# Odd layer's windowed attention: score products split into three float32r matmuls, the two heads alternating on the row halves, and the maps normalised on VectorE

## The chip, the cores and the metric

The program runs on one core of one Trainium2 chip. The metric is the device time of one execution in microseconds (us), lower is better. The engines are named as in the profile: PE (TensorE matmul), PEld (its weight load), DVE (VectorE), ACT (ScalarE), POOL (GpSimd) and SP (SyncE, whose queue issues most transfers).

## The reference

One step of a two-layer trunk over 128 context tokens and 256 latent tokens of 1024 features, in float32. The odd layer's mixer, which the change touches, is a windowed attention with 16 query heads, 4 key and value heads of 64 features, and one extra logit per head (the sink):

```python
q, k, v = jnp.split(h @ w_in, [...], axis=-1)
q = _rms_norm(q.reshape(b, s, C_HEADS, HEAD_DIM), qk_g[0])
k = _rms_norm(k.reshape(b, s, C_KV_HEADS, HEAD_DIM), qk_g[1])
...
s_c = jnp.einsum("bqgrd,bcgd->bgrqc", qi, k_ctx) * scale      # cached context keys
s_l = jnp.einsum("bqgrd,bkgd->bgrqk", qi, ks) * scale         # latent keys, rotated
s_l = jnp.where(valid, s_l, -jnp.inf)                         # |query - key| <= 128
p = jax.nn.softmax(jnp.concatenate([s_c, s_l, sink], axis=-1), axis=-1)
o = p_c @ v_ctx + p_l @ v_lat
```

Context tokens attend only to their own 128 keys. The rest of each layer is two half SwiGLU blocks and, in the even layer, another attention; none of that is changed.

## The kernel before

All 384 tokens stay on the chip, feature-major. Weights stream in tiles of up to 1 MB through the SP queue into three `raw` buffers and are split into a high and a low float32r part (`wh` by ACT, line 80; `wl` by DVE or POOL, line 84). A projection is then three float32r matmuls for each 128 rows (`mm3`, lines 178 to 180). The odd mixer has a start and a pipeline.

**The start.** `odd_mixer` makes keys and the first queries (u = 0), then the values, then rotates the two key tiles `kt[0]`, `kt[1]` (`finish_keys`) and copies them with their halves of the partitions swapped into `kt[2]`, `kt[3]` by four transfers. Then it rotates the first queries (`rope`, four DVE instructions, lines 706 to 710) and calls `advance(8)`. `advance` runs pieces of the products of the other queries (u = 1, 2, 3, each with two chunks c); a finished product is squared and copied by ACT (`hsq`, `oq`, lines 721 and 722), its rows of sums are made by PE (`rows`, line 679), brought to columns (`cols`, line 691), and its latent part is rotated.

**The pipeline.** It has 24 steps (u, c, i): two query heads, which lie on the two halves of the partitions, and one tile i of 128 queries. For i = 0 there are 128 keys, for i = 1 and 2 there are 384; three steps with the same u and c are called a triple here. In the program's order, step s has: the scores of s on PE (`s`, line 1202, and a mask added by a matmul with an identity, line 1208); on DVE two maxima `omx` (line 1214), then `ong`, `oes` (lines 1216 to 1222) and for the step before `ors` (lines 1234, 1235); on ACT two exponentials `e` (line 1226) and `oes`; on POOL the product of the maps of s - 1 with their factors (line 1236); `fill(s)`, which is pieces of the query products, and from step 18 of the output product `down`; the transposes `aT` of s - 3 (line 1246) and their copies `at_sb` on ACT (line 1248); the products `oo` with the values for s - 4 (line 1259), which after i = 2 are split into `gh` (ACT, line 1266) and `gl` (DVE, line 1267); and half a weight tile of splitting (`refill_half`). Each engine works through its own list in this order, which is fixed when the program is built.

## Time and profile before

| what | value |
|---|---|
| time, median of 3 runs | 1532.3 us (1532.04 to 1536.19) |
| span of the profiled execution | 1533.8 us |
| its mean granted TensorE clock | 0.989 |
| PE busy, DVE busy, ACT busy, POOL busy | 1496.8, 1087.1, 665.4, 188.5 us |
| first score matmul of the odd layer, first `oo` | 1117.0 us, 1133.9 us |
| last score matmul, last `oo` | 1207.1 us, 1220.7 us |

The profiled execution's span is 1.5 us above the median of the timed runs. Times within the execution are counted from the start of its span. A busy PE is not a PE at its peak, since matmuls are pipelined and their ends are modelled.

### The profile page before, as it was taken

What the parts mean: (1) busy time and instruction counts of PE and PEld (TensorE: products, weight loads), DVE (VectorE), ACT (ScalarE), POOL (GpSimd) and SP (SyncE); (2) the same over time, 40 slices, a digit from 0 to 9 for tenths busy, and PEclk for the clock granted to TensorE, in tenths of its full rate; (3) what the DMA queues carried; (4) which work ended last, traced back from release to release, by engine and by line L of the source; (5) the groups of instructions that cost most, each with busy time, mean ns of one, the idle gap of its engine ahead of it and who ended that gap; (6) DMA issues with size and microseconds to landing.
All of it is one profiled execution on the core that took longest, in us unless ns stands there. A gap on an engine that the chain in (4) does not pass through costs nothing.

```text
span 1533.8 us, 22554 instructions
## 1 busy us (share of the span) xinstructions
PE 1496.8 (98%) x8938; PEld 1419.5 (93%) x8938; DVE 1087.1 (71%) x1723; ACT 665.4 (43%) x1218; POOL 188.5 (12%) x120
## 2 busy tenths in 40 slices
PE   7989999999999999999999999999999999999998
PEld 5888999999899999999999999999965799999998
DVE  2799888868786887787779868876785386444432
ACT  3653333366555642334454333325565564232331
POOL 2450000005322100000010000000453230000000
PEclk9999999999999999999999999999997999999999
DMA  9767677642323376576536656743320034433431
GB/s 292 233 221 234 226 242 259 220 151 90 110 83 124 116 255 220 179 246 221 178 110 218 223 179 222 243 165 111 109 74 29 4 111 137 138 98 127 142 102 41
DMA packets 204555, 248.60 MB, mean 162 GB/s; under 512 B 5957, under 2 KB 186786, under 8 KB 204450
## 3 DMA queue, kind: packets, MB, share of 16 engines
q1 hardware_dynamic: 203374, 245.79, 48.6%
q8 instruction: 70, 1.15, 0.3%
q10 hardware_dynamic: 1076, 1.38, 0.3%
q14 instruction: 35, 0.29, 0.1%
HBM read 244.26 MB, written 2.36 MB: 161 GB/s over the span
## 4 chain that ended last, share of the span: by engine, by line
PE 85%; DVE 7%; ACT 3%; issue 2%; POOL 1%; DMA 1%; SPq 0%; ACTq 0%; DVEq 0%; POOLq 0%
PE proj L178 17%; PE proj L180 17%; PE proj L179 17%; PE down L179 8%; PE down L178 8%; PE down L180 8%; PE s L1202 2%; DVE wl L84 2%; PE m_sum L269 1%; PE oo L1259 1%; ACT wh L80 1%; PE aT L1246 1%; DVE acc L354 1%; DVE macc L228 1%; DVE x L359 1%
## 5 line engine op out<-in xcount | busy, mean ns | idle before, releaser
L178 PE MATMUL proj<-xh,wh 128*128 128x384 f32 (+1 forms) x1648 | 562.8, 342 | 1.1 <-ACT xh L391 1.1
L179 PE MATMUL proj<-xl,wh 128*128 128x384 f32 (+1 forms) x1648 | 556.8, 338 | 2.3 <-DVE xl L463 2.2
L180 PE MATMUL proj<-xh,wl 128*128 128x384 f32 (+1 forms) x1648 | 556.1, 337 | 0.0
L84 DVE TENSOR_TENSOR wl<-raw,wh 128x1024 fp32r<-128x1024 f32 (+1 forms) x292 | 352.6, 1246 | 131.2 <-ACT wh L80 130.6
L80 ACT ACTIVATE wh<-raw 128x1024 fp32r<-128x1024 f32 (+1 forms) x330 | 317.3, 1012 | 150.9 <-PE down L179 81.8
L178 PEld LDWEIGHTS proj<-xh,wh 128*128 128x128 f32 x1648 | 310.4, 188 | 16.2 <-issue 9.5
L179 PEld LDWEIGHTS proj<-xl,wh 128*128 128x128 f32 x1648 | 310.9, 189 | 3.6 <-DVE xl L463 3.2
L180 PEld LDWEIGHTS proj<-xh,wl 128*128 128x128 f32 x1648 | 310.4, 188 | 0.0
L178 PE MATMUL down<-gh,wh 128*128 128x384 f32 x832 | 280.8, 337 | 8.2 <-ACT gh L628 8.2
L179 PE MATMUL down<-gl,wh 128*128 128x384 f32 x832 | 279.3, 336 | 1.6 <-DVE gl L629 1.6
L180 PE MATMUL down<-gh,wl 128*128 128x384 f32 x832 | 278.6, 335 | 0.0
L221 DVE SCALAR_TENSOR_TENSOR macc<-wm,cpad,macc 128x1024 f32<-128x1024 f32 x210 | 259.1, 1278 | 0.3 <-issue 0.3
L178 PEld LDWEIGHTS down<-gh,wh 128*128 128x128 f32 x832 | 156.4, 188 | 11.6 <-ACT gh L628 8.8
L179 PEld LDWEIGHTS down<-gl,wh 128*128 128x128 f32 x832 | 156.4, 188 | 3.6 <-DVE gl L629 3.3
L180 PEld LDWEIGHTS down<-gh,wl 128*128 128x128 f32 x832 | 156.4, 188 | 0.0
L628 ACT ACTIVATE gh<-gf 128x768 fp32r<-128x768 f32 x44 | 37.3, 848 | 262.2 <-DVE gf L618 256.9
L359 DVE SCALAR_TENSOR_TENSOR x<-down,m,x 128x128 f32<-128x128 f32 x224 | 82.5, 411 | 72.9 <-PE down L180 72.9
L611 ACT ACTIVATE sg<-proj 128x384 f32<-128x384 f32 x78 | 37.8, 488 | 147.2 <-PE proj L180 147.1
L84 POOL TENSOR_TENSOR wl<-raw,wh 128x1024 fp32r<-128x1024 f32 (+1 forms) x38 | 82.7, 2189 | 134.1 <-ACT wh L80 105.4
L618 DVE TENSOR_TENSOR gf<-proj,sg 128x384 f32<-128x384 f32 x78 | 43.2, 554 | 68.4 <-PE proj L180 68.4
L189 POOL TENSOR_TENSOR nr<-nv,neghalf 128x3 f32<-128x3 f32 x6 | 5.1, 853 | 573.0 <-DVE nv L418 573.0
L629 DVE TENSOR_TENSOR gl<-gf,gh 128x768 fp32r<-128x768 f32 x44 | 42.2, 958 | 40.2 <-ACT gh L628 40.2
(212 smaller groups left out, 1168.5 us busy)
## 6 DMA issues: line engine op xcount, KB each, us to landing
raw<-in_ffn_w SPq DMA_DIRECT2D x117, 1024.0 KB, 5.3
wm<-in_w_mod SPq DMA_DIRECT2D x128, 512.0 KB, 4.1
raw<-in_ffn_w SPq DMA_DIRECT2D x16, 768.0 KB, 5.9
raw<-in_even_w_in SPq DMA_DIRECT2D x12, 1024.0 KB, 5.2
wm<-in_w_mod SPq DMA_DIRECT2D x24, 256.0 KB, 6.1
raw<-in_odd_w_in SPq DMA_DIRECT2D x6, 1024.0 KB, 4.8
raw<-in_even_w_out SPq DMA_DIRECT2D x4, 1024.0 KB, 5.0
raw<-in_odd_w_out SPq DMA_DIRECT2D x4, 1024.0 KB
```

What stands on the lines that cost most here:

```text
L80: self.k.nc.scalar.activation(parts[0][:, a:b], raw[:, a:b], AF.Copy)
L84: engine.tensor_tensor(out=lo[:, a:b], in0=raw[:, a:b], in1=h[:, a:b].bitcast(F32), op=ALU.subtract)
L178: mm(out, w[0], x[0], start=first, stop=False)
L179: mm(out, w[0], x[1], start=False, stop=False)
L180: mm(out, w[1], x[0], start=False, stop=last)
L221: nc.vector.scalar_tensor_tensor(out=acc, in0=t, scalar=c, in1=acc, op0=ALU.mult, op1=ALU.add)
L359: self.nc.vector.scalar_tensor_tensor(out=self.x[oc][:, a:b], in0=psum[:, a:b], scalar=gate[:, oc, g:g + 1], in1=self.x[oc][:, a:b], op0=A ...
L611: nc.scalar.activation(sg[c], out[:, 0:T], AF.Silu)
L618: nc.vector.tensor_tensor(out=gf[:, c], in0=out[:, 0:T], in1=sg[c], op=ALU.mult)
L628: nc.scalar.activation(gh[:, at:at + 2], gf, AF.Copy)
L629: nc.vector.tensor_tensor(out=gl[:, at:at + 2], in0=gf, in1=gh[:, at:at + 2].bitcast(F32), op=ALU.subtract)
L1202: nc.tensor.matmul(s[p][:, 0:n], qs[u][hs, c, i * P:(i + 1) * P], keys[p][hs, k0:k0 + n], start=True, stop=(i == 0),)
```

## The change

The queries and keys of the odd layer's attention are split into float32r parts. `kh`, `kl` hold the two key tiles, `kh2`, `kl2` the swapped ones; each query product goes to a scratch tile (`oqf`, for u = 0 `q0`), is rotated there, and then ACT writes its high part (line 1105 of the new kernel) and DVE its low part (line 1106); `key_parts` does the same for keys (lines 1178, 1179). The score of a step is then three float32r matmuls for each head, in an order that alternates between the two heads, and both masks follow behind them (lines 1230, 1237). The maps are multiplied by their factors with two DVE instructions (line 1266) and no longer on POOL. The four swapping transfers are issued from the SP queue. `fill` calls `advance(1)` in every step, the output product begins at step 17 and goes on at every other step, and the new keys' output (`nk`) is made ahead of the pipeline. The parts lie in buffers that the modulation's stream used; for this the accumulator `macc` moves to another pool.

```diff
     def odd_mixer(self, l):
         okt = self.mix.tile([P, 4, 512], F32, tag="kt", name="okt")
         kt = [okt[:, i] for i in range(4)]
+        kh, kl, kh2 = [self.wpool.tile([P, 2, 512], F32R, tag="wm", name="okp", bufs=3) for _ in range(3)]
+        kl2 = self.wpool.tile([P, 2, 512], F32R, tag="wp", name="okp", bufs=1)
...
-        qs[0] = self.mix.tile([P, 2, T], F32, tag="q", name="oq", bufs=2)
-        sqq = [self.first_squares(tiles[2 + j], self.odd_g[:, 0:1], qs[0][:, j], j) for j in range(2)]
+        def query_tiles(u):
+
+            if u == 2:
+                t = self.mix.tile([P, 2, 2, T], F32R, tag="kt", name="oq")
+                return [t[:, 0], t[:, 1]]
+            pool, tag = (self.wpool, "macc") if u == 1 else (self.mix, "q")
+            return [pool.tile([P, 2, T], F32R, tag=tag, name="oq", bufs=2) for _ in range(2)]
+
+        def query_parts(u, c, t):
+            h, lo = qs[u]
+            nc.scalar.activation(h[:, c], t, AF.Copy)
+            nc.vector.tensor_tensor(out=lo[:, c], in0=t, in1=h[:, c].bitcast(F32), op=ALU.subtract)
+
+        q0 = [self.c3("q0"), self.c3("q0")]
+        sqq = [self.first_squares(tiles[2 + j], self.odd_g[:, 0:1], q0[j], j) for j in range(2)]
...
             yield from self.project_pieces(c, res, 2)
-            sq = self.scaled_and_squares(res[0], self.odd_g[:, 0:1], qs[u][:, c], c)
+            full[u, c] = self.c3("oqf")
+            sq = self.scaled_and_squares(res[0], self.odd_g[:, 0:1], full[u, c], c)
...
             def rope(u, c):
-                self.rope(qs[u][:, c, TC:T], qs[u][:, c, TC:T])
+                t = full.pop((u, c))
+                if c == 0:
+                    qs[u] = query_tiles(u)
+                self.rope(t[:, TC:T], t[:, TC:T])
+                query_parts(u, c, t)
...
         for j in range(2):
             self.finish_keys(ksc[:, j], rk, j, kt[j])
+            nc.sync.dma_start(out=kt[2 + j][0:64], in_=kt[j][64:128])
+            nc.sync.dma_start(out=kt[2 + j][64:128], in_=kt[j][0:64])
+
+        def key_parts(h, lo, j, t):
+            nc.scalar.activation(h[:, j], t, AF.Copy)
+            nc.vector.tensor_tensor(out=lo[:, j], in0=t, in1=h[:, j].bitcast(F32), op=ALU.subtract)
+
...
+        qs[0] = query_tiles(0)
         for j in range(2):
-            nc.scalar.dma_start(out=kt[2 + j][0:64], in_=kt[j][64:128])
-            nc.scalar.dma_start(out=kt[2 + j][64:128], in_=kt[j][0:64])
+            self.rope(q0[j][:, TC:T], q0[j][:, TC:T])
+            query_parts(0, j, q0[j])
+            key_parts(kh, kl, j, kt[j])
         for j in range(2):
-            self.rope(qs[0][:, j, TC:T], qs[0][:, j, TC:T])
+            key_parts(kh2, kl2, j, kt[2 + j])
         advance(8)
...
+        new_keys()
         def fill(s):
-            advance((1, 2, 2, 1, 1)[s] if s < 5 else 1)
-            if s == 20:
-                new_keys()
-            if s == 18:
+            advance(1)
+            if s == 17:
                 out.append(self.out_start(gs, order, ("mm", "at", "at", "at"), 1))
-            if 18 <= s < 22 or s >= 24:
+            if s in (17, 19, 21, 23) or s >= 24:
                 next(out[0][2], None)
...
-            for p in range(2):
-                hs = slice(64 * p, 64 * p + 64)
-                nc.tensor.matmul(
-                    s[p][:, 0:n], qs[u][hs, c, i * P:(i + 1) * P], keys[p][hs, k0:k0 + n],
-                    start=True, stop=(i == 0),
-                )
-                if i:
-                    m0 = 256 if i == 1 else 128
+            for a, b in ((0, 0), (1, 0), (0, 1)):
+                for p in range(2):
+                    hs = slice(64 * p, 64 * p + 64)
+                    nc.tensor.matmul(
+                        s[p][:, 0:n], qs[u][a][hs, c, i * P:(i + 1) * P],
+                        keys[p][b][hs, u // 2, k0:k0 + n], start=(a + b == 0), stop=(i == 0 and b == 1),
+                    )
+            if i:
+                m0 = 256 if i == 1 else 128
+                for p in range(2):
                     nc.tensor.matmul(
                         s[p][:, m0:m0 + P], self.ident16, self.masks[i - 1], start=False, stop=True
                     )
...
             nc.vector.reciprocal(rs, rs)
-            nc.gpsimd.tensor_tensor(
-                out=e[:, :, 0:n], in0=e[:, :, 0:n], in1=rs.unsqueeze(2).to_broadcast([P, 2, n]), op=ALU.mult
-            )
+            for p in range(2):
+                nc.vector.tensor_scalar(
+                    out=e[:, p, 0:n], in0=e[:, p, 0:n], scalar1=rs[:, p:p + 1], scalar2=None, op0=ALU.mult
+                )
...
-        self.macc = [keep.tile([P, D], F32, name=f"macc{g}") for g in range(2)]
+        self.macc = [self.wpool.tile([P, D], F32, tag="macc", name="macc", bufs=2) for _ in range(2)]
```

How the lists of the engines change at the start is read from the order of the built programs. On ACT, before, the list between the output of the values and the first exponentials is this (`hsq` and `oq` are the squares and the copy of the products of u = 1, first chunk 0, then chunk 1; `rows_sb` is the copy that follows PE's `rows`):

```order
L1155 DMA out_odd_v<-ov_9819 128x256
L1159 DMA okt<-okt 64x512
L1160 DMA okt<-okt 64x512
L1159 DMA okt<-okt 64x512
L1160 DMA okt<-okt 64x512
L721 ACTIVATE hsq<-proj 128x384
L722 ACTIVATE oq<-proj,cols 128x384
L721 ACTIVATE hsq<-proj 128x384
L722 ACTIVATE oq<-proj,cols 128x384
L682 ACTIVATE rows_sb<-rows 64x384
L80 ACTIVATE wh<-raw 128x1024 x2
```

The same place on ACT in the changed kernel (`oq` is now the high part of a query, `okp` that of a key):

```order
L1181 DMA out_odd_v<-ov_9823 128x256
L1105 ACTIVATE oq<-q_10041 128x384
L1178 ACTIVATE okp<-okt 128x512
L1105 ACTIVATE oq<-q_10042 128x384
L1178 ACTIVATE okp<-okt 128x512 x3
L721 ACTIVATE hsq<-proj 128x384
L722 ACTIVATE oqf<-proj,cols 128x384
L1105 ACTIVATE oq<-oqf 128x384
L721 ACTIVATE hsq<-proj 128x384
L722 ACTIVATE oqf<-proj,cols 128x384
L1105 ACTIVATE oq<-oqf 128x384
L682 ACTIVATE rows_sb<-rows 64x384
```

Six copies now stand ahead of the first `hsq`, and the high part of chunk 0 stands ahead of the second `hsq`; the four transfers are gone from this list. On DVE, before, four rotations of queries follow one another (u = 0, then u = 1, each with chunks 0 and 1; the first and the last of each rotation's four rows are shown), then the column factors, a weight split and the first maxima:

```order
L696 TENSOR_SCALAR orq_v<-cols 128x12
L706 STREAM_SHUFFLE rope_s<-oq 128x256
...
L710 TENSOR_TENSOR oq<-rope_c,rope_s 128x256
...
L696 TENSOR_SCALAR orq_v<-cols 128x12
L84 TENSOR_TENSOR wl<-raw,wh 128x1024
L1214 TENSOR_REDUCE omx<-s 128x1 x2
```

The same place on DVE in the changed kernel:

```order
L710 TENSOR_TENSOR q_10041<-rope_c,rope_s 128x256
L1106 TENSOR_TENSOR oq<-q_10041,oq 128x384
L1179 TENSOR_TENSOR okp<-okt,okp 128x512
...
L710 TENSOR_TENSOR q_10042<-rope_c,rope_s 128x256
L1106 TENSOR_TENSOR oq<-q_10042,oq 128x384
L1179 TENSOR_TENSOR okp<-okt,okp 128x512 x3
...
L710 TENSOR_TENSOR oqf<-rope_c,rope_s 128x256
L1106 TENSOR_TENSOR oq<-oqf,oq 128x384
```

Every rotation is now followed by a subtraction that reads ACT's copy of the same tile, and four subtractions of keys stand ahead of the rotations of u = 1. On PE the list at this place keeps its order, with `nk` and the six small score matmuls at its end:

```order
L679 MATMUL rows<-hsq,con 32x384 x2
L178 MATMUL proj<-xh,wh 128x384
L179 MATMUL proj<-xl,wh 128x384
L180 MATMUL proj<-xh,wl 128x384
...
L691 MATMUL cols<-con,rows_sb 128x64 x3
L1197 MATMUL nk<-con,okt 128x128 x2
L1230 MATMUL s<-okp,oq 128x128 x6
```

The three rows of a query product come four times, twelve float32r matmuls; the `rows` of u = 1, which read both `hsq`, still stand ahead of everything that leads to the first scores.

## Rows read from the trace of the kernel before

**Rows 1.** The page's parts 1 and 4: busy time of each engine in the whole span, with its share and its instructions, and the chain of work that ended last by engine.

```profile
PE 1496.8 (98%) x8938; PEld 1419.5 (93%) x8938; DVE 1087.1 (71%) x1723; ACT 665.4 (43%) x1218; POOL 188.5 (12%) x120
...
PE 85%; DVE 7%; ACT 3%; issue 2%; POOL 1%; DMA 1%; SPq 0%; ACTq 0%; DVEq 0%; POOLq 0%
```

**Rows 2.** Busy time of each engine in two stretches of the pipeline, about a triple each. Columns: the stretch, its length, busy time of PE, PEld, DVE, ACT and POOL with instructions, granted clock, DMA share and GB/s.

```profile
1127.00:1139.00 12.00, 12.00 (x68) 7.47 (x69) 10.87 (x30) 8.38 (x25) 5.88 (x4) 1.00 0.05 15
1139.00:1151.00 12.00, 12.00 (x86) 8.12 (x83) 7.48 (x29) 8.48 (x30) 6.72 (x5) 1.00 0.27 87
```

**Rows 3.** The chain of work that ended last, one triple of steps at the full clock. Columns: start, time on the chain, engine, tile and line.

```profile
1139.39 0.42 PE s L1202 x4
...
1142.25 0.84 PE s L1202 x2
1143.09 0.16 PE s L1208
...
1144.25 0.23 PE proj L178
1144.48 0.18 PE proj L179
...
1145.36 0.66 PE aT L1246 x6
...
1150.15 0.81 PE oo L1259 x12
1150.96 0.42 PE s L1202 x4
```

**Rows 4.** Timeline of ACT between the rotated keys and the first scores. Columns: start, duration, engine, line, operation and tiles; in brackets the engine's idle time before it and what ended that.

```profile
1109.57 0.88 ACTq L1159 DMA_DIRECT2D okt<-okt  x1
...
1112.45 0.49 ACT L721 ACTIVATE hsq<-proj 128x384 f32<-128x384 f32 x1 [2.95 <-DVE oq L710]
```

**Rows 5.** Timeline of PE at the same place.

```profile
1111.46 0.34 PE L180 MATMUL proj<-xh,wl 128*128 128x384 f32 x1
1113.00 1.68 PE L679 MATMUL rows<-hsq,con 128*32 128x384 f32 x4 [1.20 <-ACT hsq L721]
...
1117.03 0.37 PE L1202 MATMUL s<-okt,oq 64*128 64x128 f32 x1
```

**Rows 6.** Timeline of DVE at the same place: the first rotation's first and last row, the weight split, and the first step's row of maxima and `ong`.

```profile
1110.75 0.44 DVE L706 STREAM_SHUFFLE rope_s<-oq 128x256 f32<-128x256 f32 x1
...
1112.22 0.43 DVE L706 STREAM_SHUFFLE rope_s<-oq 128x256 f32<-128x256 f32 x1
...
1117.43 1.22 DVE L84 TENSOR_TENSOR wl<-raw,wh 128x1024 fp32r<-128x1024 f32 x1
1118.57 0.48 DVE L1214 TENSOR_REDUCE omx<-s 128x1 f32<-128x128 f32 x2
...
1119.35 0.16 DVE L1218 SCALAR_TENSOR_TENSOR ong<-omx,negsink 128x2 f32<-128x2 f32 x1
```

**Rows 7.** Granted clock of PE in four stretches: two early in the program, two in the middle of the pipeline. Columns: the stretch, its length, PE busy with instructions, granted clock, DMA share and GB/s.

```profile
109.00:117.20 8.20, 0.64 (x5) 0.82 0.69 220
117.60:121.00 3.40, 3.10 (x18) 0.50 0.13 52
1168.90:1172.40 3.50, 1.60 (x8) 1.00 0.23 68
1172.40:1189.40 17.00, 16.94 (x74) 0.50 0.14 50
```

**Rows 8.** Timeline of DVE in a step of the pipeline.

```profile
1160.41 0.16 DVE L1216 TENSOR_TENSOR omx<-omx,orq 128x2 f32<-128x2 f32 x1
...
1161.17 0.43 DVE L706 STREAM_SHUFFLE rope_s<-oq 128x256 f32<-128x256 f32 x1
1161.51 1.66 DVE L708 TENSOR_TENSOR rope_c<-oq,con 128x256 f32<-128x256 f32 x1
...
1167.81 0.56 DVE L1267 TENSOR_TENSOR gl<-oo,gh 128x384 fp32r<-128x384 f32 x1 [1.44 <-ACT gh L1266]
1168.28 1.01 DVE L1214 TENSOR_REDUCE omx<-s 128x1 f32<-128x384 f32 x2
```

**Rows 9.** Timeline of ACT in the same stretch.

```profile
1160.89 0.67 ACT L1226 ACTIVATE e<-s,ong,orq 128x384 f32<-128x384 f32 x1
...
1162.66 0.85 ACT L1248 ACTIVATE at_sb<-aT 128x384 f32<-128x384 f32 x2
```

**Rows 10.** The instructions of one line of the even layer's attention, which multiply maps by a column on DVE: count, then minimum, median and maximum in ns, first and last start, forms.

```profile
L983 DVE TENSOR_SCALAR e<-e,rs x12: 278/410/414, 404.2 to 454.3; 128x384 f32<-128x384 f32 x8, 128x128 f32<-128x128 f32 x4
```

**Rows 11.** Timeline of POOL while DVE takes the second step's maxima.

```profile
1120.74 2.39 POOL L84 TENSOR_TENSOR wl<-raw,wh 128x1024 fp32r<-128x1024 f32 x1
```

**Rows 12.** The instructions of one line: `omx` on DVE in all 24 steps, minimum, median and maximum in ns.

```profile
L1216 DVE TENSOR_TENSOR omx<-omx,orq x24: 160/161/1687, 1119.2 to 1208.4; 128x2 f32<-128x2 f32 x24
```

**Rows 13.** The chain of work that ended last, a stretch of the pipeline in which the granted clock is 0.50.

```profile
1177.78 1.58 PE s L1202 x2
...
1181.37 1.28 PE aT L1246 x6
```

**Rows 14.** Timeline of DVE: `ong` of the last step.

```profile
1208.60 0.16 DVE L1218 SCALAR_TENSOR_TENSOR ong<-omx,negsink 128x2 f32<-128x2 f32 x1
```

**Rows 15.** Timeline of PE: the last `oo`.

```profile
1220.38 0.61 PE L1259 MATMUL oo<-at_sb,ov 128*64 128x128 f32 x8
```

More of the change, by code (lines that the diff above doesn't have):

```diff
@@ L1090, in odd_mixer @@
         qs, rq = {}, {}
-        qs[0] = self.mix.tile([P, 2, T], F32, tag="q", name="oq", bufs=2)
-        sqq = [self.first_squares(tiles[2 + j], self.odd_g[:, 0:1], qs[0][:, j], j) for j in range(2)]
+        def query_tiles(u):
[10 more added lines that the diff above has]
+        sqq = [self.first_squares(tiles[2 + j], self.odd_g[:, 0:1], q0[j], j) for j in range(2)]
         self.w.done(2, False)
+        full = {}
         def project(u, c):
-            if u == 2 and c == 0:
-                t = self.wpool.tile([P, D], F32, tag="wp", name="oq2", bufs=1)
-                qs[u] = t[:, 0:2 * T].rearrange("p (c t) -> p c t", c=2)
-            elif c == 0:
-                qs[u] = self.mix.tile([P, 2, T], F32, tag="q", name="oq", bufs=2)
             res = []
             yield from self.project_pieces(c, res, 2)
-            sq = self.scaled_and_squares(res[0], self.odd_g[:, 0:1], qs[u][:, c], c)
+            full[u, c] = self.c3("oqf")
+            sq = self.scaled_and_squares(res[0], self.odd_g[:, 0:1], full[u, c], c)
             if c:
@@ L1194, in scores @@
         def scores(u, c, i):
-            keys = [kt[u // 2 + (0 if p == u % 2 else 2)] for p in range(2)]
+            keys = [kt[0 if p == u % 2 else 2:][:2] for p in range(2)]
             s = [self.ps("at", "s"), self.ps("at", "s")]
```

2 lines of the change are left out of this document (1 added, 1 removed).

## The prediction, made before the changed kernel was run

> **What bounds the kernel now.** The page comes first: PE is busy for 98% of the span and carries 85% of the chain that ended last; DVE carries 7% of it [rows 1]. PE work removed therefore counts, as long as no other engine becomes the pace where it is removed. The busy times by stretch answer that for the pipeline: PE is busy throughout, and DVE, the busiest of the others, for 7.5 to 10.9 of 12 us [rows 2]. So it has 1.1 to 4.5 us of room in about a triple. The chain shows one triple: it takes 1150.96 - 1139.39 = 11.57 us, in which a 384-key head costs 0.84 for its score and 0.16 for its mask, both heads of a 128-key step 0.42, six float32r matmuls of a fill 1145.36 - 1144.25 = 1.11, a step's transposes 0.66 and its products with the values 0.81 [rows 3]. The timelines of the start come next: ACT issues transfers from 1109.57 and starts `hsq` only at 1112.45 [rows 4], and PE stands still for 1.20 us until it is there [rows 5]. The first scores are at 1117.03 [rows 5], the first `ong` at 1119.35 [rows 6] and the last at 1208.60 [rows 14], so the pipeline's 23 steps take 89.25 us. From there to the end of the last `oo` at 1220.38 + 0.61 [rows 15] PE has the output product to do, and its work there stays the same. I sum over these three parts.
>
> **Scores on PE.** A float32r matmul of 384 columns takes about 0.18, from 1.11 / 6 [rows 3]. Three passes over two heads are, if the row halves run side by side, 3 x 0.18 plus the 0.2 by which a score now exceeds its streaming, about 0.72; one after another they are 6 x 0.18 + 0.1 = 1.2. The rows favour the first: both heads of 128 keys take 0.42, while a third of 0.84 for each would be 0.56 in series [rows 3]. Two masks in a row cost between 0.16 and 0.32; I take 0.22. A 384-key step falls from 2.00 to 0.94, a 128-key step stays near 0.45. Over 16 long steps PE loses 17 us of work; in series it would lose 16 x 0.5 = 8.
>
> **The pace of the pipeline.** A triple then holds on PE 2 x 0.94 + 0.45 for scores, about 1.5 for transposes, 2.0 for `oo` and 3.3 for three fills: 9.2 us with fills, 6 without. On DVE it holds maxima 2 x 1.01 + 0.48 [rows 6, 8], three times five small rows of 0.76 together, from 1160.41 to 1161.17 [rows 8], the new multiplies and `gl` 0.56. The even layer's multiplies of this shape take 0.41 and 0.28 [rows 10]; a pair back to back, overlapping by some 0.05, is 0.74 and 0.48, so 1.96 a triple. The sum is 7.3 us. To it come: `gl`'s wait for ACT, 1.44 before [rows 8], about 0.9 after since a multiply fills part of it; four query chunks that are rotated inside the pipeline, each with 1112.22 - 1110.75 = 1.47 [rows 6], a wait of about 0.6 for ACT's copy, as `hsq` of such a tile takes 0.49 [rows 4], and 0.47 for the low part; two weight splits of 1.15 [rows 6]. So 7.3 x 23 / 3 + 6 x 0.9 + 4 x 2.54 + 2.3 = 73.9 us. Two things are added. First a loop: `ong` of a step, its two exponentials (1.3, from 0.67 each) and the copies `at_sb` behind them (0.85) [rows 9], the next transposes and `oo` (0.7 and 0.8) [rows 3], scores (0.95) and the maxima with `omx` (1.3) [rows 8] return to `ong` two steps later after 5.9 us, 3.0 a step, where DVE's own work in a step without rotation is 2.5 to 2.6. For some 12 steps that is 0 to 6; I take 4. Second POOL: an `omx` of 0.16 took 1.69 [rows 12] beside POOL's weight split of 2.39 [rows 11], a rotation's 0.42 row 1.66 [rows 8]. Some splits remain: 0 to 5, taken 3. The pipeline comes to 81 us, 8 less than now. DVE and its loop are the pace, not PE; half of PE's 17 us is not collected.
>
> POOL's multiply of the maps is gone, and with it POOL's time before the transposes; that is off the sum, since the transposes of a step come three steps later.
>
> The Trainium skill, SBUF — State Buffer, section "Who interferes with whom", says that DVE and GpSimd share one port pair as an exclusive lock for a whole instruction, and that `tensor_scalar` in its two-port modes takes part in it. By that the new multiplies could block behind POOL's weight splits too, up to about 2 us a time, and the removed multiply on POOL would free other rows. The slow `omx` [rows 12] agrees with the lock; the even layer's twelve multiplies, none above 414 ns [rows 10], show no case of it.
>
> **The start.** In the new list of ACT four high parts of keys (one for each tile and swapped tile) and two of queries stand ahead of the first `hsq` of u = 1, and the high part of the first rotated chunk stands ahead of the second `hsq`. PE's four `rows` read one `hsq` after the other, and all of PE's later work stands behind them. DVE feeds ACT here and is fed by it: from 1110.75 it makes a rotation (1.5), the low part behind ACT's copy (0.5 each), and the low part of a key behind ACT's copy of that (0.6 for 512 columns, half of the 1.22 for 1024 [rows 6]), and all again for the second chunk. Step by step I get: first query rotated 1112.3, its copy 1112.9, key copy 1113.35, low parts 1114.1; second query 1115.5, copies 1116.1 and 1116.6, low parts 1117.3; swapped keys 1118.5; then the rotation of u = 1 to 1120.0, its copy 1120.6, the second `hsq` 1121.05. The first `hsq` goes ahead of that copy, at 1117.5, so half of `rows` (0.84 of the 1.68 [rows 5]) falls into PE's gap; the other half starts at 1121.05, where it now starts at 1113.84, 7.2 us later. Behind it the same twelve matmuls, columns and scores follow: the first scores come near 1124.6 and the first maxima, behind the weight split, some 7.5 us later than now. Behind a gap of PE the clock can fall: early in the program PE was busy for 0.64 of 8.20 us, and the next 3.40 us were granted 0.50 [rows 7]. Twelve matmuls at half clock cost some 2 us more, of which part hides behind DVE: 1.3. So the start is +8.8. The swapping transfers, now issued by SP from about 1108.8, are needed at 1116.5; 7 us are enough for transfers that ACT issued in 2.8 us, so I cost them at nothing; late by 1 us they would cost 1 us. The lower end is DVE's own list without any wait for PE: from 1110.75 four rotations (5.9), four low query parts with their waits (4.3), four low key parts (2.4), the columns and the split (1.3) end at 1124.7, against 1118.57 [rows 6]: +6.1.
>
> **Sum.** +8.8 - 8.2 = +0.6, on a span of 1533.8, which lies 1.5 above the median of the timed runs (1532.3): 1532.9, taken 1533.0. Half-done fills shift work between the pipeline and the tail and change the sum by 0.5 at most.
>
> **Rivals.**
> - Faster. `gl`'s wait, the loop and POOL's locks do not add up but hide in each other: the pipeline takes 73.5 to 76, and the clock stays at full level. Then -14 + 8 = -6.5: about 1526. For it: PE has little work left in the unfilled steps, so a late row is caught up. Against it: DVE's idle rows of now are waits of this very loop. It decides if a step without rotation takes 2.6 us, not 3.0.
> - Slower, by the clock. Where PE was busy for 1.60 of 3.50 us, the next 17 us were granted 0.50 [rows 7], and a score took 1.58 and the transposes 1.28 instead of 0.84 and 0.66 [rows 13]. The new pipeline leaves PE idle more often, some 3 us in an unfilled triple. At half clock a filled triple would hold 9.2 x 1.9 = 17 us of PE, an unfilled one 11. If two stretches of 17 us fall to this level, each costs 2.7 to 6.6 us, and the time is about 1540. It decides if a gap of PE such as that row's comes again in the unfilled steps.
> - Slower, without overlap. The halves run in series or 128-column float32r products are dear: PE is the pace again in filled steps with 10.3 us a triple, +4 us: 1537.
>
> **How the numbers follow.** A measurement can tell a change of about 0.3%, 4.6 us. The forecast, 1528 to 1537.5, has 0.44; the faster rival 0.28; the slower one by the clock 0.20; by missing overlap 0.08. The last two together give 0.28 for slower, since a mild case of them stays within 0.3% as often as the forecast's upper end leaves it. The range reaches from 1524.5, where the faster rival meets the lower bound of the start, to 1541.5, where both clock stretches fall in.
>
> **What would show it.** Right: PE idle for some 8 us ahead of the second half of `rows`, near 1121; first `ong` near 1127 to 1128; last `ong` 81 us behind it; a long step's scores on PE at 0.7 with two masks of 0.2; DVE waiting little. Wrong: an `rows` that starts before 1116 (the list was not what held it), a pipeline under 77 us, or a granted clock of 0.50 for more than 10 us inside it. The second multiply of a pair above 1 us would show a lock that the sum has only as bounds.

## The result, and the profile after

The changed kernel takes 1547.57 us (median, 1547.4 to 1549.96) against 1532.17 of the kernel before in the same session: 1.0104 times as long, 95% interval 1.0091 to 1.0116, 15.4 us more. The forecast was 1533.0 with a range up to 1541.5. It missed on the slow side.

The page of the changed kernel, parts 1 and 4, beside [rows 1]:

```profile
PE 1489.9 (96%) x8986; PEld 1424.1 (92%) x8986; DVE 1105.7 (71%) x1783; ACT 672.1 (43%) x1230; POOL 160.2 (10%) x96
...
PE 81%; DVE 9%; ACT 4%; issue 2%; DMA 2%; POOL 1%; SPq 0%; ACTq 0%; DVEq 0%; POOLq 0%
```

PE lost 7 us of busy time, where the forecast had 17 us of work less: part of what is left runs at half clock, as a table below shows. Its share of the chain fell from 85% to 81%, and DVE, ACT and the transfers gained 4 points. Timelines of DVE at both ends of the pipeline, the first and the last `ong`, beside [rows 6, 14]:

```profile
1130.70 0.48 DVE L1243 TENSOR_REDUCE omx<-s 128x1 f32<-128x128 f32 x2
...
1131.48 0.16 DVE L1247 SCALAR_TENSOR_TENSOR ong<-omx,negsink 128x2 f32<-128x2 f32 x1
...
1132.46 1.02 DVE L1243 TENSOR_REDUCE omx<-s 128x1 f32<-128x384 f32 x2 [0.62 <-PE s L1237]
1133.51 1.77 DVE L1245 TENSOR_TENSOR omx<-omx,orq 128x2 f32<-128x2 f32 x1
```

```profile
1221.96 0.16 DVE L1247 SCALAR_TENSOR_TENSOR ong<-omx,negsink 128x2 f32<-128x2 f32 x1
```

So the pipeline's 23 steps take 90.48 us, where they took 89.25, and start 12.13 us later. Of that, 1.84 us had come about long before: the even layer's values, at 371 us, already start 1.84 us later in this execution. This is a difference between executions and not of the change: a run shown below that has neither the new start nor the moved accumulator (e9) has the same 1.84, and one with the moved accumulator (e10) has 0.43. The start itself costs 10.3 us, and everything behind the last `ong` 0.7: 1.84 + 10.3 + 1.2 + 0.7 = 14.0, the difference of the spans, 1547.8 - 1533.8.

The start on DVE, the end of the second query's rotation and the low parts of keys:

```profile
1116.99 0.42 DVE L710 TENSOR_TENSOR q<-rope_c,rope_s 128x256 f32<-128x256 f32 x1
...
1118.52 0.69 DVE L1179 TENSOR_TENSOR okp<-okt,okp 128x512 fp32r<-128x512 f32 x1
1120.12 1.34 DVE L1179 TENSOR_TENSOR okp<-okt,okp 128x512 fp32r<-128x512 f32 x2 [0.91 <-ACT okp L1178]
```

The same place on ACT and PE, beside [rows 4, 5]:

```profile
1119.46 1.28 ACT L1178 ACTIVATE okp<-okt 128x512 fp32r<-128x512 f32 x2 [0.97 <-DMA okt<-okt]
1120.64 0.47 ACT L721 ACTIVATE hsq<-proj 128x384 f32<-128x384 f32 x1
...
1123.26 0.52 ACT L1105 ACTIVATE oq<-oqf 128x384 fp32r<-128x384 f32 x1 [1.68 <-DVE oqf L710]
1123.69 0.47 ACT L721 ACTIVATE hsq<-proj 128x384 f32<-128x384 f32 x1
```

```profile
1121.17 1.49 PE L679 MATMUL rows<-hsq,con 128*32 128x384 f32 x2 [7.52 <-ACT hsq L721]
1124.22 1.49 PE L679 MATMUL rows<-hsq,con 128*32 128x384 f32 x2 [1.56 <-ACT hsq L721]
```

PE stands still for 7.52 us ahead of the first half of `rows` and 1.56 us ahead of the second, each time for ACT's `hsq`. The copies of the swapped keys, which stand ahead of both, waited 0.97 us for the transfers. Granted clock in the start and in three stretches of the pipeline, beside [rows 7]:

```profile
1112.00:1118.00 6.00, 1.65 (x10) 0.99 0.71 205
1118.00:1128.00 10.00, 5.27 (x11) 0.50 0.01 4
1142.00:1148.00 6.00, 5.97 (x26) 0.50 0.00 0
1163.00:1169.00 6.00, 5.59 (x26) 0.50 0.00 1
1191.00:1201.00 10.00, 8.26 (x52) 0.50 0.34 107
```

One stretch at 0.50 lies in the start and three in the pipeline, 27 us of it in all by the trace, where the profiled execution before had one of 17 us in the pipeline and none in the start. The chain that ended last shows a long step's scores as forecast, 0.72 for six products, with 0.18 of masks on the chain, beside [rows 3]:

```profile
1176.06 0.72 PE s L1230 x6
1176.78 0.18 PE s L1237
```

The new multiplies, and `omx`, beside [rows 10, 12]; POOL beside [rows 11]:

```profile
L1266 DVE TENSOR_SCALAR e<-e,ors x48: 280/414/422, 1136.0 to 1224.5; 128x384 f32<-128x384 f32 x32, 128x128 f32<-128x128 f32 x16
```

```profile
L1245 DVE TENSOR_TENSOR omx<-omx,orq x24: 160/161/2370, 1131.3 to 1221.8; 128x2 f32<-128x2 f32 x24
```

```profile
1132.88 2.39 POOL L84 TENSOR_TENSOR wl<-raw,wh 128x1024 fp32r<-128x1024 f32 x1
1156.10 2.38 POOL L84 TENSOR_TENSOR wl<-raw,wh 128x1024 fp32r<-128x1024 f32 x1 [20.84 <-ACT wh L80]
...
1191.99 2.34 POOL L84 TENSOR_TENSOR wl<-raw,wh 128x1024 fp32r<-128x1024 f32 x1 [26.01 <-ACT wh L80]
```

The multiplies cost what the even layer's did. `omx`, which takes 0.16, took 1.77, 2.37 and, in step 14, 1.81 us in the three steps in which POOL splits weights: 5.5 us more in all.

### The profile page after: what moved, and what is told of

The parts are those of the page before. It is cut to its first block, busy times and chain, and to the rows that moved or that the text cites. A ratio compares the mean times of both kernels' runs of the same rounds, so it can differ in the third digit from the quotient of the medians.

```text
span 1547.8 us, 22674 instructions
## 1 busy us (share of the span) xinstructions
PE 1489.9 (96%) x8986; PEld 1424.1 (92%) x8986; DVE 1105.7 (71%) x1783; ACT 672.1 (43%) x1230; POOL 160.2 (10%) x96
## 4 chain that ended last, share of the span: by engine, by line
PE 81%; DVE 9%; ACT 4%; issue 2%; DMA 2%; POOL 1%; SPq 0%; ACTq 0%; DVEq 0%; POOLq 0%
PE proj L178 17%; PE proj L180 16%; PE proj L179 16%; PE down L179 8%; PE down L178 8%; PE down L180 8%; DVE wl L84 2%; PE m_sum L269 1%; ACT wh L80 1%; DVE acc L354 1%; PE s L1230 1%; ACT e L1255 1%; PE oo L1289 1%; DVE macc L228 1%; DVE omx L1243 1%
```

## The experiments

Eighteen runs, told in the order in which they ran. The table has, for each, the first `ong`, the pipeline (first to last `ong`) in the profiled execution, the median, and the ratio to the kernel before with its interval. Step s is the time from `ong` of step s - 1 to that of step s. A first `ong` also holds what an execution had lost or won long before it, as the 1.84 us above; by the same count that is between -0.3 and +1.8 us in the other runs, and the text takes it off where it matters.

| run | first `ong` | pipeline | median | ratio, 95% interval |
|---|---|---|---|---|
| before | 1119.35 | 89.25 | 1532.2 | |
| after | 1131.48 | 90.48 | 1547.6 | 1.0091 to 1.0116 |
| e1 rows first | 1124.43 | 91.62 | 1543.6 | 1.0062 to 1.0093 |
| e2 split on DVE | 1129.55 | 83.32 | 1540.9 | 1.0045 to 1.0075 |
| e3 maps on POOL | 1130.17 | 84.29 | 1543.3 | 1.0058 to 1.0088 |
| e4 heads serial | 1128.85 | 90.24 | 1548.0 | 1.0092 to 1.0125 |
| e5 = e1 + e2 | 1124.37 | 88.12 | 1540.3 | 1.0037 to 1.0067 |
| e6 = e5 + e3 | 1123.81 | 86.92 | 1539.0 | 1.0031 to 1.0061 |
| e7 before, maps on DVE | 1120.54 | 85.43 | 1533.1 | 0.9998 to 1.0017 |
| e8 more products | 1129.25 | 90.90 | 1548.1 | 1.0092 to 1.0122 |
| e9 = e7, split on DVE | 1122.84 | 83.39 | 1532.2 | 0.9991 to 1.0010 |
| e10 = e9, new scores in half | 1121.17 | 87.12 | 1536.2 | 1.0021 to 1.0043 |
| e11 = e2, no rotation | 1130.84 | 78.46 | 1536.6 | 1.0019 to 1.0041 |
| e12 = e2, late parts | 1130.92 | 80.95 | 1540.3 | 1.0041 to 1.0071 |
| e13 = e2, copies first | 1130.59 | 81.52 | 1538.4 | 1.0026 to 1.0052 |
| e14 = e13, start spread | 1122.71 | 90.55 | 1538.7 | 1.0024 to 1.0054 |
| e15 = e13, maps on POOL | 1129.64 | 80.64 | 1538.0 | 1.0022 to 1.0046 |
| e16 = e14, maps on POOL | 1121.94 | 89.80 | 1538.9 | 1.0026 to 1.0059 |
| e17 = e2, no low parts | 1131.37 | 77.14 | 1535.5 | 1.0011 to 1.0030 |
| e18 = e2, products in the gap | 1129.19 | 83.91 | 1541.2 | 1.0038 to 1.0074 |

The first theory was that the order of ACT's list costs the start 10 us and that POOL's locks, with the falls of the clock behind them, cost the pipeline its gain. The rival was that DVE's added work is what counts, wherever it stands.

**e1, rows first.**

```diff
...
             self.rope(q0[j][:, TC:T], q0[j][:, TC:T])
-            query_parts(0, j, q0[j])
-            key_parts(kh, kl, j, kt[j])
+        advance(8)
+        for j in range(2):
+            query_parts(0, j, q0[j])
+            key_parts(kh, kl, j, kt[j])
         for j in range(2):
             key_parts(kh2, kl2, j, kt[2 + j])
-        advance(8)
...
-                query_parts(u, c, t)
+                later.append([(8, 5)[c] if u == 1 else 1, query_parts, (u, c, t)])
```

> The changed kernel, but at the start ACT makes both hsq of u = 1 and rows_sb before any high part, and the parts of u = 1 are made in steps 0 and 1. Theory (the order of ACT's list holds rows): first ong falls from 1131.5 to about 1124, the total from 1547.6 to about 1540 (-7). Rival (DVE's own list and the late swapping transfers, which land at 1119.4, hold the first scores anyway): first ong at 1129 or later, total -1 to -3.

Measured: -4.0 us, and first `ong` at 1124.43, near the theory's 1124; but 1.5 of these 7 us are the early difference of the two executions, so the start wins 5.5. The pipeline grew by 1.1: the first two steps, which now hold the parts of u = 1, take 2.1 us more, although one locked `omx` fewer stands in the pipeline (two slow rows, 2.00 and 1.45 us, instead of three). Between the two.

**e2, weight splits on DVE.**

```diff
+        self.light = False
         self.w.refill()
...
         self.pipeline(*self.odd_attention(qs, rq, (kh, kl, kh2, kl2), vt, gs), 3, fill, self.w.refill_half)
+        self.light = True
```

> The changed kernel, but every weight split from the start of the pipeline to its end runs on DVE, none on POOL. Theory (POOL's split locks omx for 1.6 to 2.2 us in three steps, PE runs dry and the clock falls behind it): -4 to -7 us, fewer stretches of granted clock 0.50. Rival (DVE's load is the pace): DVE gets three splits of 1.15 more, +1 to +3 us.

Measured: -6.7 us; the pipeline falls to 83.32, although DVE makes two splits more in it, 2.3 us (the third now stands ahead of the first `ong`). `omx` in this run:

```profile
L1247 DVE TENSOR_TENSOR omx<-omx,orq x24: 160/160/161, 1129.3 to 1212.7; 128x2 f32<-128x2 f32 x24
```

None of the 24 is over 161 ns. (This execution has a fall of the clock of its own, in steps 21 and 22: they take some 2 us more than in e11, e12, e17 and e18, which is to be kept in mind where its pipeline is compared.) Each of the two added splits, 1.22 us long, makes its step (7 and 15) 1.14 us longer. The locks are shown: taking away what locks takes away 7.2 us of pipeline, 9.5 with the added splits counted.

**e3, maps on POOL.** The two DVE multiplies give way to the old instruction on POOL.

```diff
-            for p in range(2):
-                nc.vector.tensor_scalar(
-                    out=e[:, p, 0:n], in0=e[:, p, 0:n], scalar1=rs[:, p:p + 1], scalar2=None, op0=ALU.mult
-                )
+            nc.gpsimd.tensor_tensor(
+                out=e[:, :, 0:n], in0=e[:, :, 0:n], in1=rs.unsqueeze(2).to_broadcast([P, 2, n]), op=ALU.mult
+            )
```

> The changed kernel, but the maps are multiplied on POOL as before. Theory (locks and clock): POOL is busy 1.5 us in each long step again and locks DVE's two-input instructions, 0 to +4 us. Rival (the multiplies on DVE are what makes DVE the pace): 2 us less of DVE in each triple, -6 to -10 us.

Measured: -4.3 us, pipeline 84.29, though `omx` is slow again:

```profile
L1245 DVE TENSOR_TENSOR omx<-omx,orq x24: 160/160/1764, 1130.0 to 1214.3; 128x2 f32<-128x2 f32 x24
```

Nine rows of DVE, four of them `omx`, are longer than their like in this pipeline, 9.9 us together. Neither as the theory (0 to +4) nor as much as the rival (-6 to -10). Whether DVE's shorter list did it or the clock, granted at 0.94 in this pipeline against 0.85 in the changed kernel's, the run does not tell.

**e4, heads serial.**

```diff
-            for a, b in ((0, 0), (1, 0), (0, 1)):
-                for p in range(2):
+            for p in range(2):
+                for a, b in ((0, 0), (1, 0), (0, 1)):
```

> The changed kernel, but the three products of head 0 stand ahead of those of head 1, so the row halves do not alternate. If alternation lets the halves overlap, a long step's six products take 1.1 to 1.2 us here and 0.72 in the changed kernel. Theory (PE is not the pace of the pipeline): total 0 to +3. Rival (PE's work decides): 16 x 0.5 = +8.

Measured: +0.4 us, no difference. But the premise fell too. The chain of this run has

```profile
1173.20 0.73 PE s L1230 x6
1173.93 0.18 PE s L1237
```

0.73 for six products, as in the alternating order: the halves overlap in either order. So the run says nothing on PE's weight in the total.

**e5, both e1 and e2.**

> Both edits of e1 and e2 in the changed kernel: hsq and rows_sb ahead of the high parts, and no weight split on POOL in the pipeline. Theory (start and locks are separate costs, -4.0 and -6.7 us apart): together about -10 us, 1537. Rival (the start's parts only move into the pipeline, where DVE is the pace): no better than e2 alone, 1541.

Measured: 1540.3, as e2 alone. The first `ong` is 5.2 us earlier (6.5 without the early difference) and the pipeline 4.8 us longer, 4.5 of it in steps 1 and 2. The rival holds: the parts mostly moved.

**e6, e5 with the maps on POOL.**

> e5 with the maps multiplied on POOL as in the kernel before. Theory (DVE's list is the pace of the steps that remain, so its multiplies count): 2 us of DVE in each triple leave, -4 us against e5: about 1533. Rival (POOL's multiply locks rotations and omx again for about as much): 0 to +4 against e5.

Measured: -1.3 against e5, intervals that overlap. Not told apart. Here too the shorter list comes with locks: five slow rows, 4.7 us together, where e5 has none.

**e7, the kernel before with the multiplies alone** (the edit of e3 the other way).

> The kernel before with one part of the change alone: the maps multiplied by two DVE instructions. The old scores keep PE busy. Theory (DVE's load counts only where PE has room): -1 to +2 us against the kernel before. Rival (the multiplies on DVE are dear wherever they stand): +4 to +8.

Measured: +1.0, interval -0.3 to +2.6 us: same. Where the old scores keep PE at work, the multiplies are free.

**e8, more products.** Six, not twelve as the expectation counts, a step, 24 in all.

```diff
             advance(1)
+            if 13 <= s <= 16:
+                junk = self.ps("mm", "proj")
+                for k in range(2):
+                    xh, xl = self.xs[k]
+                    self.mm3(junk[:, 0:T], (xh[:, 0:P], xl[:, 0:P]), (xh[:, 0:T], xl[:, 0:T]), k == 0, k == 1)
```

> The changed kernel with twelve more float32r products of 384 columns (four times 1.1 us at the full clock, into a tile that nobody reads) in each of the steps 13 to 16, where no query product is left. Theory (the falls of the clock behind PE's gaps cost time there): the granted clock stays higher between 1185 and 1204, and although PE has more to do the total is -1 to -4 us. Rival (the clock is not what costs in these steps): 0 to +4.

Measured: +0.5, no difference. Granted clock from `ong` of step 13 to that of step 17, in the changed kernel and in this run:

```profile
1186.62:1204.74 18.12, 13.74 (x86) 0.62 0.19 59
```

```profile
1184.58:1202.92 18.34, 15.06 (x111) 0.91 0.18 59
```

The clock is 0.91 instead of 0.62, and the steps take as long: what it returned, the added products took (24 of 0.18 are 4.4 us at the full clock), or neither was on the path. Inconclusive as to which.

**e9, the kernel before with multiplies and weight splits on DVE** (edits of e7 and e2).

> The kernel before with DVE multiplying the maps and making all low parts of weights in the pipeline, so that POOL has nothing large there. Theory (a lock by POOL opens the gap of PE behind which its clock is 0.50 for 17 us, and that costs where PE is the pace): -3 to -6 us against the kernel before. Rival (the fall of the clock costs nothing here either, as the run with more products showed for the changed kernel): -1 to +1.

Measured: no difference, 0.9991 to 1.0010. The rival holds: without POOL's locks the kernel before is no faster. It had more of them than the changed kernel: nine slow rows in its pipeline, five `omx` and four of rotations (the longest are in [rows 8, 12]), 8.0 us together against 5.5; e7 has 4.6 and e9 none. So the same locks cost 6.7 us where DVE's list is long (e2) and nothing that can be told here.

**e10, new scores in the second half only.** u = 0 and 1 keep the old scores and the old start.

```diff
...
+            for a, b in ((0, 0), (1, 0), (0, 1)) if u > 1 else ():
+                for p in range(2):
+                    hs = slice(64 * p, 64 * p + 64)
+                    nc.tensor.matmul(
+                        s[p][:, 0:n], qs[u][a][hs, c, i * P:(i + 1) * P],
+                        kp[b][hs, 0 if p == u % 2 else 1, k0:k0 + n], start=(a + b == 0), stop=(i == 0 and b == 1),
+                    )
             for p in range(2):
                 hs = slice(64 * p, 64 * p + 64)
-                nc.tensor.matmul(
+                if u < 2: nc.tensor.matmul(
...
             advance((1, 2, 2, 1, 1)[s] if s < 5 else 1)
+            if s in (2, 3):
+                parts(kh[:, s - 2], kl[:, s - 2], kt[2 * s - 3])
```

> e9, and the new float32r scores only for the second key tile, u = 2 and 3 (steps 12 to 23); u = 0 and 1 keep the old scores, so the start is that of before. The parts of keys are made in steps 2 and 3. Theory (the start's serial list costs 10 us and the pipeline gives back at most 5): against e9 -2 to -5 us, since the second half's scores lose 8.5 us of PE and nothing is added ahead of the pipeline. Rival (the loop through ACT and DVE is as long as PE's work was): 0 to +2 against e9.

Measured: +4.1 against e9. Two windows show why, e9's and e10's steps 12 to 23:

```profile
1162.54:1206.23 43.69, 40.20 (x255) 0.92 0.09 28
```

```profile
1165.49:1208.29 42.80, 34.89 (x274) 0.84 0.09 29
```

PE's busy time falls by 5.3 us (its work by 8.5, part of it at half clock), the time for the same steps by 0.9 us. Of these steps, 12 holds the parts of a query and is 1.2 us longer than e9's; the eleven others win 2.1 together. Steps 2 and 8, with such parts too, are 1.2 longer each, and steps 3 and 4, where DVE also makes the parts of the keys, take 11.9 instead of 7.7 us. So most of the scores' gain is not collected even where nothing is paid for it at the start.

**e11, no rotation.** The rotations of the queries of u = 2 and 3 are left out.

```diff
...
-                self.rope(t[:, TC:T], t[:, TC:T])
+                if u == 1:
+                    self.rope(t[:, TC:T], t[:, TC:T])
```

> e2 (weight splits on DVE) without the rotations of the queries of u = 2 and 3, four times four DVE instructions, left out; the products are computed on queries that are not rotated. Theory (in the pipeline a rotation stands in the loop from ong to the next maxima and adds its whole length): -4 x 1.5 = -6 us against e2's 1540.9. Rival (DVE waits for 20 us of the pipeline and a rotation fills those waits, as the sum on record had it for the loop): 0 to -2.

Measured: -4.3 against e2, where sixteen DVE instructions of 5.9 us together are gone. The four steps that held a rotation (2, 6, 10 and 14) are 3.4 us shorter together. So some 60 to 70% of a rotation's length is on the path: nearer to the theory than to a filled wait.

**e12, late parts.**

```diff
-                query_parts(u, c, t)
+                later.append([2, query_parts, (u, c, t)])
```

> e2, but the high and low part of a query of u = 1 to 3 are made one step after its rotation. Theory (DVE's wait for ACT's copy, 0.65 each, stands in the loop): 4 x 0.65 = -2.6 us against e2, and another -1 at the start, where the second hsq no longer waits for a copy. Rival (the wait is filled by others): 0 to -1.

Measured: -0.6, intervals overlap. Not told apart.

**e13, copies first.** `ps` is the scores on PE alone, `a` now what DVE and ACT make of them, `b` the transposes and `at_sb`:

```diff
-        self.pipeline(*self.odd_attention(qs, rq, (kh, kl, kh2, kl2), vt, gs), 3, fill, self.w.refill_half)
+        n, ps, a, m, b, c = self.odd_attention(qs, rq, (kh, kl, kh2, kl2), vt, gs)
+        for s in range(n + 4):
+            if s < n:
+                ps(s)
+            if 0 <= s - 3 < n:
+                b(s - 3)
+            if s < n:
+                a(s)
...
```

> e2 with the transposes and ACT's copies at_sb of step s - 3 placed between the scores of step s and its maxima, so that on ACT the copies stand ahead of the exponentials of the same step. Theory (the loop from ong through exponentials, copies, transposes, oo and scores back to ong paces the steps): the loop loses 2.3 of its 5.9 us in two steps, DVE's list of 2.5 to 2.6 a step becomes the pace, pipeline from 83.3 to 74 to 77, total -6 to -9 against e2's 1540.9. Rival (DVE's list is the pace already): 0 to -2.

Measured: -2.4, nearer to the rival. The pipeline is 81.52 instead of 83.32, and the difference lies in the steps in which e2 has its fall of the clock. By this run the loop through `at_sb` and `oo` is not what sets most steps.

**e14, start spread.**

```diff
...
-        advance(8)
+        advance(1)
+        first_queries(0)
+        key_parts(kh, kl, 0, kt[0])
+        advance(7)
+        key_parts(kh2, kl2, 0, kt[2])
...
+            if s == 0:
+                first_queries(1)
+            if s == 2:
+                key_parts(kh, kl, 1, kt[1])
+            if s == 4:
+                key_parts(kh2, kl2, 1, kt[3])
```

> e13, and only what the first step needs stands ahead of the pipeline: the first chunk's rotation and parts and the parts of key tile 0; the second chunk, the rotations of u = 1, the parts of key tile 1 and the rotation of the first chunk of u = 2 are spread over steps 0 to 7; the swapping transfers of tile 0 go from ACT. Theory (with the loop shortened DVE has room in the steps): first ong 8 us earlier than in e13, pipeline 3 to 5 longer, total -3 to -5 against e13. Rival (DVE's work adds its length wherever it stands): 0 to -1.

Measured: +0.3 against e13. First `ong` 7.9 earlier, pipeline 9.0 longer, 8.6 of it in steps 1 to 6. The rival, and cleanly: what leaves the start comes back in the steps.

**e15 and e16, e13 and e14 with the maps on POOL.**

> e13 with the maps multiplied on POOL. Theory (DVE's list is the pace in e13): -3 to -6 against e13. Rival (POOL's locks or another loop through the exponentials take it back): 0 to +2.

> e14 with the maps multiplied on POOL. If both theories hold: first ong near 1122, pipeline 75 to 78, total 1523 to 1527, faster than the kernel before. If both rivals hold: as e13, 1532 to 1535.

Measured: -0.4 against e13 and +0.2 against e14. Some 15 us of multiplies less on DVE (48 of 0.28 to 0.41) bring nothing where POOL makes them instead. But locks come in with them, which e13 and e14 have not:

```profile
L1263 DVE TENSOR_TENSOR omx<-omx,orq x24: 160/161/1236, 1129.4 to 1210.1; 128x2 f32<-128x2 f32 x24
```

Nine rows of DVE are slow in either pipeline, 4.8 us together in e15 and 5.4 in e16. So these runs do not tell whether the multiplies pace e13: the rival named POOL's locks, and they take back a part of it.

**e17, no low parts.** The products read the high parts in their place, so the scores are less exact.

```diff
...
             nc.scalar.activation(h[:, j], t, AF.Copy)
-            nc.vector.tensor_tensor(out=lo[:, j], in0=t, in1=h[:, j].bitcast(F32), op=ALU.subtract)
```

> e2 without the twelve low parts of queries and keys that DVE makes (eight of 0.56 us, four of 0.67); the second and third product of each score read the high parts instead, so PE, ACT and POOL have the same work. Theory (DVE's added work and its waits for ACT's copies add to the time wherever they stand): 7.2 us of DVE and its waits of some 0.6 behind each copy go, the total falls by 7 to 11 us from e2's 1540.9. Rival (the order of ACT's list and PE's own loop set the time): 0 to -3.

Measured: -5.3 against e2, all of it in the pipeline, where only four of the twelve stood, 4.8 us with the wait of 0.65 ahead of each. The steps that held them (2, 6, 10 and 14) are 3.4 us shorter together, three of them by 0.9 to 1.2 and step 10 not at all; the rest lies in steps 5, 21 and 22, in or right behind stretches where e2's clock was at 0.50. The start gained nothing, and ACT's timeline says why:

```profile
1115.18 0.61 ACT L1176 ACTIVATE okp<-okt 128x512 fp32r<-128x512 f32 x1
1117.92 1.27 ACT L1176 ACTIVATE okp<-okt 128x512 fp32r<-128x512 f32 x2 [2.13 <-DMA okt<-okt]
1119.10 0.47 ACT L721 ACTIVATE hsq<-proj 128x384 f32<-128x384 f32 x1
```

With DVE's part of the list gone, ACT waits 2.13 us for the swapping transfers and only then gets to `hsq`. Between theory and rival, and a second holder of the start is shown: the transfers end there at 1117.9.

**e18, products in the gap.** They fill PE's wait for `hsq`.

```diff
...
                 for j, sq in enumerate(sqs[u]):
+                    for k in range((12, 4)[j]):
+                        self.mm3(more[:, 0:T], (xh[:, 0:P], xl[:, 0:P]), (xh, xl), j + k == 0, j == 1 and k == 3)
                     nc.tensor.matmul(rows[32 * j:32 * j + 32, 0:T], self.sel, sq, start=True, stop=True)
```

> e2 with 36 products of 384 columns ahead of the first half of rows of u = 1 and 12 ahead of the second half, into a tile that nobody reads: they stand in the gap in which PE waits for ACT's hsq. Theory (the clock falls behind that gap, and rows and twelve products at 0.50 cost the start 1.5 to 2 us): granted clock 1.00 through the start, first ong and total -1.5 to -2 against e2. Rival (DVE's list hides PE's slower products): 0.

Measured: +0.3, no difference. Granted clock in the start, and from `ong` of step 7 to that of step 9, with e2 and e5 for the same steps:

```profile
1112.00:1126.00 14.00, 13.08 (x71) 1.00 0.20 59
1155.45:1163.96 8.51, 7.43 (x42) 0.60 0.37 124
```

```profile
1155.74:1161.62 5.88, 4.06 (x37) 1.00 0.54 177
```

```profile
1155.03:1163.38 8.35, 7.28 (x42) 0.61 0.39 125
```

The clock stays at 1.00 through the start, and the first `ong` comes 0.36 us earlier, 0.5 without the early difference, which is less than one list's starts differ between executions (9.1 to 10.3 us, below): the half clock of the start was hidden. In the pipeline the same two steps, 8 and 9, took 5.88 us at 1.00 in e2, and 8.35 and 8.51 at about 0.60 in e5 and e18. There one stretch costs some 2.5 us. None of these three runs has a lock, so such stretches come without locks too.

No version beat the kernel before; e7 and e9, which keep its scores, equal it.

## Why the prediction was wrong

The forecast's span is 1534.4 us and the measured one 1547.8. Of the 13.4 us between them, 1.8 are the early difference, 1.5 the start, 9.4 the pipeline and 0.7 what comes behind it.

**The base.** The sum was made against a span of 1533.8, put 1.5 above the median. But a run's time is 1.7 to 1.9 us more than its span in all 62 later executions of the kernel before, so the profiled one lasted near 1535.6, some 3.4 us above the median. The record places the difference: three of the 62 have a mean clock of 0.989, as the profiled one, and they are the three slowest (1535.3 to 1536.0), while the others have 0.990 to 0.994. Its stretch of 17 us at 0.50 [rows 7] is some 7 us long in e7 and e9, which time as the kernel before does and have pipelines of 85.4 and 83.4. Steps 16 to 18 in the profiled execution and in e7:

```profile
1176.45:1190.79 14.34, 14.34 (x61) 7.96 (x59) 5.46 (x23) 6.33 (x22) 3.55 (x3) 0.55 0.01 3
```

```profile
1179.17:1187.71 8.54, 8.35 (x56) 4.51 (x52) 7.15 (x29) 6.07 (x22) 0.00 (x0) 1.00 0.01 3
```

So the saving of 8 was counted from a pipeline that is usually some 4 us shorter than 89.25; this is an estimate, as only one execution of the kernel before was traced.

**The start: +8.8 forecast, +10.3 measured.** Step by step (less the early 1.84): the first query rotated at 1112.3 as forecast, the second at 1115.6 (1115.5), its key's low part done at 1117.4 (1117.3). Then the swapped keys: 1119.6 (1118.5), since the transfers, costed at nothing, came 0.97 us late. From there on everything is 1.3 later: second half of `rows` at 1122.4 (1121.05). In e3, e4 and e8, whose list is the same, ACT does not wait for the transfers and the start costs 9.1 to 9.3 without the early differences. The clock's 1.3 is not borne out: e18 gives 0.4 to 0.5, no more than the scatter. The form of the start was right, and how little it decides was not seen: e5 and e14 move it by 5 to 9 us, and the time stays.

**Scores on PE.** Right: 0.72 for the products, 0.18 for the masks. The overlap is there, but the alternation in the title is not what brings it: e4 has 0.73 without.

**The pipeline: 81 forecast, 90.5 measured.** This is the step that failed, in two terms of its sum: the wait of DVE's maxima for PE's scores ("a loop", "0 to 6; I take 4") and POOL's locks ("0 to 5, taken 3"). What ended DVE's idle time ahead of the maxima in the pipeline (us, times), in the changed kernel and in e2:

```profile
  PE s L1237: 6.3, 5
  PE s L1230: 3.7, 3
```

```profile
  PE s L1232: 3.2, 4
  PE s L1239: 3.0, 3
```

That is 10.0 us against the 4 of the loop, and the locked rows of `omx` are 5.5 against 3. The other terms came out: DVE's own rows with the short gaps between them 67.5 against 66.0, `gl`'s waits 4.9 against 5.4, the waits for ACT's copies of queries 2.6 against 2.4. All five add up to the 90.5 us, of which DVE is busy for 68.5, the locked time included:

```profile
1131.48:1221.96 90.48, 74.32 (x534) 54.05 (x534) 68.49 (x237) 55.53 (x179) 13.04 (x6) 0.85 0.11 36
```

Without the locks (e2) the wait for scores falls to 6.2, and all that the locks bring is worth 9.5 us. What makes up the 4 beyond their own rows is in part argued: a stretch at 0.50 costs 2.5 us where two runs could be compared, the sum has nothing for the clock inside the pipeline, and two of the changed kernel's three stretches there (1142 and 1163) come behind locked steps; but e5 and e18 have such stretches without a lock, and e8, where a higher clock gave nothing back in steps 14 to 17, does not confirm the price. For e2 the sum gives 73.9 + 4 + 2.3 = 80.2, and 83.3 were measured, some 2 of it behind its own fall of the clock.

The sum was right to add rotations, low parts and splits to DVE's list one behind the other: 60 to 70% of a rotation counts (e11), 3.4 of 4.8 us of the low parts with their waits (e17), nearly the whole of a split (e2), and the start's parts lengthen the steps by most of what the start wins (e5, e14). In a step these rows stand in DVE's list between one `ong` and the next maxima. So what the prediction first called room, DVE's 1.1 to 4.5 idle us in about a triple, is not free for such rows. "DVE and its loop are the pace, not PE; half of PE's 17 us is not collected" named the right engine and stopped too early: next to none of it is collected, and e10 is the plainest case. The sign of being wrong that the prediction named came too: 0.50 for more than 10 us inside the pipeline.

**The rivals.** The slower one by the clock gave 1540, with two stretches of 17 us; three came, shorter, 27 us in all. It put them down to PE's idle time; that two of them follow locks was not in it, and its price of 2.7 to 6.6 per stretch is 2.5 for one of 7 us where it could be read. The faster one (its -14 + 8 is -6, not -6.5) asked for a pipeline of 73.5 to 76, which no run has; the shortest is e17's 77.1. Missing overlap did not come.

**The locks.** The second `omx` waited beside POOL's row at 1132.88, while the maxima beside the same row took 1.02 us for two, as in [rows 8]. The Trainium skill, SBUF — State Buffer, section "Who interferes with whom", has it so: a DVE instruction with two SBUF inputs contends with a GpSimd instruction that reads SBUF, a `tensor_reduce` does not; the trace agrees. That the new multiplies could be locked too is not shown by any run here: none of them ran beside a weight split of POOL, since `omx` stood ahead of them and was blocked first, and none of the 48 took over 422 ns.

**What stays open.** What paces e13 and e15 alike, at 81 us of pipeline, is not settled: not the loop through the copies alone, and the multiplies can't be judged beside the locks that come with them on POOL. Nor is it shown why the clock falls in one step and not in another, or how much of the 10.0 us of waits for scores it makes.

## What to carry to other kernels

Work taken off an engine that was 98% busy was worth nothing here, because the work that replaced it lies on an engine that feeds the first through a loop: add up that engine's list with every row that stands in it, price its waits for the other engines by a trace and not by a guess, and don't count its idle time as room. Before a saving is taken from a profiled execution, put that execution's own time and clock beside the median. A small instruction at the head of a chain is the one to check for a shared port: 0.16 us became 2.37. And a lock has no price of its own: removing such locks brought 6.7 us where DVE was the pace and nothing where PE was.

## What the runs showed of the hardware that was not expected

Two row halves of PE overlap whether their products alternate or not: 0.72 and 0.73 us for six (after, e4). Ten microseconds at a granted clock of 0.50 cost 0.5 us at most in the start (e18 against e2), while seven cost 2.5 in the pipeline (e5 and e18 against e2): it depends on who waits. Transfers between the halves of the partitions, 128 KB each, issued on the queue of the weight loads behind three of these, were awaited until 8.2 us after the issue (the chain of the changed kernel):

```profile
1111.20 8.18 DMA okt<-okt
```
